# Every store through `store()` is begun by GpSimd's queue instead of SyncE's in a one-core decoder block

## The chip, the cores and the metric

The kernel runs on one core of one Trainium2 chip. The metric is the device time of one execution in microseconds (us); before the change its median over three runs is 2041.13 us. Five engines work side by side: TensorE (PE, its weight loads listed as PEld), VectorE (DVE), ScalarE (ACT), GpSimd (POOL) and SyncE (SP). A DMA is begun by an instruction in the queue of one of them and then carried out by 16 DMA engines that all queues share.

## The reference

One decoder layer for x of shape (1, 2048, 1024) in float32. Two token mixers read the same normalised input, one output projection joins them, then follows a gated feed-forward network with 2816 hidden columns:

```python
h  = rmsnorm(x, g1)
p  = h @ w_in                      # q, k, v, g, a, cb, cc, ch
la = log_sigmoid((a @ w_gate_up + b_gate)) / 16
oA = rmsnorm_head(gla_chunked(q, k, v, la)) * silu(g)   # 4 heads, 64 x 128 state
oB = cb * conv3(cc * ch)           # causal, depthwise, width 3
x1 = x + concat(oA, oB) @ w_out
h2 = rmsnorm(x1, g2)
x2 = x1 + (silu(h2 @ w_gate) * (h2 @ w_up)) @ w_down
out = rmsnorm(x2, gf)
```

`gla_chunked` carries a state over chunks: S_t = diag(exp(la_t)) S_(t-1) + k_t v_t^T, o_t = q_t S_t.

## The kernel before

The 2048 positions are four blocks of 512 (`PB`), and two blocks make a *half*. The large products (input projection, feed-forward up and down) run as *units*: a 2 x 2 arrangement of quadrants of weights and activations that is computed with seven products instead of eight, from sums and differences of the quadrants (`PRODUCTS`: A11 B11, S1 T1, S2 T2, A12 B21, S3 T3, S4 B22, A22 T4). Each float32 operand is split into a high and a low part of the type fp32r (`split`: ACT makes the high part at L194, DVE the low part at L195), so that one product over 128 rows is three matmuls, L484 to L486 in `product_step`:

```python
pe.matmul(o[:], wh, xh, ...)
pe.matmul(o[:], wh, xl, ...)
return pe.matmul(o[:], wl, xh, ...)
```

A finished bank of PSUM is copied out by ACT (L530) or added to an earlier sum by DVE (L518). The output projection (L1273 to L1276) splits its operands in the same way but is not a unit.

In the order of time the stages are: an opening up to about 50 us; the input projection of half 0 to about 250 us; that of half 1, with the recurrent mixer (GLA) in its background, to about 550 us; the output projection of half 0 and, from about 664 us, of half 1; the feed-forward network of half 0 (about 760 to 1400 us) and of half 1 (to about 2005 us); the rest is the last unit, with the final norm.

The on-chip memory does not hold the activations of a stage, so each stage writes what it makes to scratch tensors in device memory and the next reads it back in the layout that it needs:

- `siT`, `siB`: normalised inputs of the input projection, as quadrants and their sums, `op` when read back
- `sk`, `sv`, `sg`, `sd`: q and k, v, gate and decay for the GLA; `kq`, `vt`, `gt`, `ee` when read back by chunk
- `sgla`, `sm`: outputs of the two mixers, each as a high and a low part; `op` when the output projection reads them
- `sx`: x1 and the partial sums of the feed-forward part; `shT`, `shB`: normalised inputs of the feed-forward part; `sa_T`, `sa_B`: its hidden activations

Every such write goes through the helper `store` (L150), every read and every fetch of weights (`raw`) through the helper `load` (L147), and both begin the DMA on `nc.sync`, SyncE's queue:

```python
def load(dst, src):
    return nc.sync.dma_start(dst, src)
def store(dst, src):
    return nc.sync.dma_start(dst, src)
```

A queue works strictly in order: an instruction that waits holds up all behind it. A store waits until its data are computed; a load waits until the buffer that it fills is free and, if it reads a scratch tensor, until the store has landed. DMAs also share eight completion counters ("lanes") in turn, so that a DMA waits for the one eight places earlier of the same group to have landed. The order on each queue is not written by hand: the tile framework's scheduler fixes the order of each engine's instructions when the kernel is built, from its own estimate of when each can start, and sets the waits between engines.

Of 1239 DMAs that SP begins, 429 come from `store`. They are 128 rows of 2 KB each (256 KB, most of them), 128 rows of 4 KB (512 KB, `so` into `sa` and `sh`), and for `sgla` 512 rows of 512 bytes (256 KB, L1237). In the last unit the output is written by direct calls (L1579), not by `store`. GpSimd itself computes little: some masks at the start and ten operations at L1577 in the last unit.

Of the kernel before, what the change touches and what calls it, by code (L numbers as in the profile page):

```python
# [53 lines left out]
def tile_hymba_block(ctx, tc, x, xt, win, wa, wgu, wout, wffn, wdown, wdown_first, small, out):  # L54
    nc = tc.nc
    act, dve, pool, pe = nc.scalar, nc.vector, nc.gpsimd, nc.tensor
# [91 lines left out]
        return nc.sync.dma_start(dst, src)  # L148

    def store(dst, src):  # L150
        return nc.sync.dma_start(dst, src)

    last_hi, last_lo, raw_loads, last_exp = [], [], [], []
    last_out = []
# [474 lines left out]
    def opening():  # L629
# [170 lines left out]
        def out(u, j, r):  # L800
            c, acc = tt("c"), o[u, j, r]
            if j:
                queued(act, lambda: act.activation(c[:], acc[:], AF.Copy))
            else:
                queued(dve, lambda: dve.tensor_tensor(c[:], acc[:], rb0[:], ALU.mult))
            store(s_kq[j][2 * u + r][:], c[:])
# [138 lines left out]
    def h1_ahead():  # L945

        def put(n, k, h):
            if n in WHOLE:
                store(s_h1[n][k][:], h[:])
                return  # L950
            hi, lo = [bx[0].tile([P, PB], F32R, name=e, tag="b") for e in ("hi", "lo")]
            split(h[:], hi[:], lo[:])
            for e, y in enumerate((hi, lo)):
                store(s_h1[n][k][:, e, :], y[:].bitcast(F32))

        for b in (2, 3):
            rb = []
            yield from rows_rstd(squares[b][:, :, 0], rb)
            rbs[b] = rb[0]
        yield from combine(lambda k, j: xt[2 + j, :, k, :], C_G1, (rbs[2], rbs[3]), put)  # L960
# [846 lines left out]
```

## Time and profile before

| | |
|---|---|
| median of three runs | 2041.13 us |
| the three runs | 2041.13, 2042.61, 2038.8 us |
| profiled execution | 2040.97 us |
| its span in the trace | 2039.2 us |
| granted clock of TensorE, mean | 0.997 |
| DVE busy | 1534.0 us (75% of the span) |
| ACT busy | 966.0 us (47% of the span) |
| bytes moved by DMA | 422.51 MB |

The span runs from the first to the last instruction that the trace holds. The profiled execution's own time is 1.77 us longer than its span; that part lies around it. "Busy" counts the computing instructions of an engine: the instructions by which SP begins DMAs appear as rows of SPq and are not in these shares.

### The profile page before, as it was taken

What the parts mean: (1) busy time and instruction counts of PE and PEld (TensorE: products, weight loads), DVE (VectorE), ACT (ScalarE), POOL (GpSimd) and SP (SyncE); (2) the same over time, 40 slices, a digit from 0 to 9 for tenths busy, and PEclk for the clock granted to TensorE, in tenths of its full rate; (3) what the DMA queues carried; (4) which work ended last, traced back from release to release, by engine and by line L of the source; (5) the groups of instructions that cost most, each with busy time, mean ns of one, the idle gap of its engine ahead of it and who ended that gap; (6) DMA issues with size and microseconds to landing.
All of it is one profiled execution on the core that took longest, in us unless ns stands there. A gap on an engine that the chain in (4) does not pass through costs nothing.

```text
span 2039.2 us, 26918 instructions
## 1 busy us (share of the span) xinstructions
PE 2019.6 (99%) x9299; PEld 1659.4 (81%) x9299; DVE 1534.0 (75%) x2763; ACT 966.0 (47%) x1915; POOL 10.3 (1%) x17
## 2 busy tenths in 40 slices
PE   9999999999999999999999999999999999999998
PEld 8788877887888788888888888887888888888886
DVE  7888967659744697777777688887777767778886
ACT  6664455656533344444444452334534444454345
POOL 0000000000000000000000000000000000000001
PEclk9999999999999999999999999999999999999999
DMA  7356885524675983546545576577444434486653
GB/s 263 119 202 222 290 299 172 163 74 158 247 245 173 373 293 134 192 151 217 181 145 191 215 287 249 187 276 279 161 165 170 161 144 170 174 331 223 248 217 129
DMA packets 190887, 422.51 MB, mean 207 GB/s; under 512 B 20032, under 2 KB 67360, under 8 KB 181280
## 3 DMA queue, kind: packets, MB, share of 16 engines
q1 hardware_dynamic: 190032, 420.15, 58.2%
q8 instruction: 73, 1.20, 0.2%
q10 hardware_dynamic: 720, 0.66, 0.1%
q14 instruction: 62, 0.51, 0.1%
HBM read 276.02 MB, written 144.70 MB: 206 GB/s over the span
## 4 chain that ended last, share of the span: by engine, by line
PE 94%; DMA 2%; DVE 2%; ACT 1%; issue 0%; SPq 0%; POOL 0%; POOLq 0%; ACTq 0%; DVEq 0%
PE mm L484 26%; PE mm L486 26%; PE mm L485 26%; PE mm L1273 3%; PE mm L1274 3%; PE mm L1276 3%; PE a_ps L1008 1%; PE mm L789 1%; PE mm L791 1%; PE o_ps L1181 1%; PE mm L790 1%; PE mm L1594 1%; PE sc L1156 1%; PE o_ps L1188 1%; DMA op<-shT 0%; PE kv L1196 0%
## 5 line engine op out<-in xcount | busy, mean ns | idle before, releaser
L484 PE MATMUL mm<-op,wq 128*128 128x512 f32 x2443 | 951.4, 392 | 7.2 <-ACT op L194 4.1
L485 PE MATMUL mm<-op,wq 128*128 128x512 f32 x2443 | 950.2, 390 | 0.5 <-DVE op L195 0.5
L486 PE MATMUL mm<-op,wq 128*128 128x512 f32 x2443 | 940.5, 390 | 0.3
L194 ACT ACTIVATE wq<-raw 128x512 fp32r<-128x512 f32 (+2 forms) x612 | 356.8, 588 | 590.1 <-PE mm L486 469.9
L484 PEld LDWEIGHTS mm<-op,wq 128*128 128x128 f32 x2443 | 459.0, 188 | 108.8 <-ACT op L194 5.4
L486 PEld LDWEIGHTS mm<-op,wq 128*128 128x128 f32 x2443 | 458.9, 188 | 96.5 <-DVE wq L195 1.1
L485 PEld LDWEIGHTS mm<-op,wq 128*128 128x128 f32 x2443 | 459.1, 188 | 96.1 <-DVE op L195 2.4
L195 DVE TENSOR_TENSOR wq<-raw,wq 128x512 fp32r<-128x512 f32 (+2 forms) x612 | 385.4, 635 | 173.5 <-ACT wq L194 171.9
L518 DVE TENSOR_TENSOR c<-mm,c 128x512 f32<-128x512 f32 x196 | 134.7, 687 | 81.6 <-PE mm L486 72.0
L518 DVE TENSOR_TENSOR y<-mm,y 128x512 f32<-128x512 f32 x185 | 126.6, 687 | 53.8 <-PE mm L486 53.2
L530 ACT ACTIVATE c<-mm 128x512 f32<-128x512 f32 x198 | 115.4, 589 | 34.7 <-PE mm L486 30.6
L436 DVE TENSOR_TENSOR raw<-raw 128x512 f32<-128x512 f32 (+2 forms) x182 | 113.3, 628 | 2.1
L194 ACT ACTIVATE wq<-s 128x512 fp32r<-128x512 f32 (+2 forms) x96 | 56.3, 587 | 108.8 <-PE mm L486 95.7
L1273 PE MATMUL mm<-op,wq 128*128 128x512 f32 x256 | 101.1, 397 | 0.1
L1274 PE MATMUL mm<-op,wq 128*128 128x512 f32 x256 | 100.0, 391 | 0.0
L1276 PE MATMUL mm<-op,wq 128*128 128x512 f32 x256 | 82.3, 390 | 0.0
L436 DVE TENSOR_TENSOR s<-raw 128x512 f32<-128x512 f32 (+2 forms) x91 | 57.3, 629 | 27.3 <-DMA raw<-in_wffn_dram 19.7
L195 DVE TENSOR_TENSOR op<-op 128x512 fp32r<-128x512 f32 x94 | 62.1, 683 | 4.0 <-ACT op L194 3.9
L195 DVE TENSOR_TENSOR wq<-s,wq 128x512 fp32r<-128x512 f32 (+2 forms) x96 | 60.8, 633 | 1.9 <-ACT wq L194 1.0
L194 ACT ACTIVATE op<-op 128x512 fp32r<-128x512 f32 x94 | 54.9, 621 | 8.0 <-DMA op<-sa_T 4.3
L436 DVE TENSOR_TENSOR raw<-s,raw 128x512 f32<-128x512 f32 (+2 forms) x91 | 57.3, 630 | 1.3
L1273 PEld LDWEIGHTS mm<-op,wq 128*128 128x128 f32 x256 | 48.1, 188 | 11.8 <-issue 1.4
(231 smaller groups left out, 1610.2 us busy)
## 6 DMA issues: line engine op xcount, KB each, us to landing
raw<-in_wffn_dram SPq DMA_DIRECT2D x44, 1024.0 KB, 6.4
sa_B<-so SPq DMA_DIRECT2D x47, 512.0 KB, 4.2
op<-sa_B SPq DMA_DIRECT2D x47, 512.0 KB, 6.8
raw<-in_win_dram SPq DMA_DIRECT2D x22, 1024.0 KB, 5.8
sa_T<-so SPq DMA_DIRECT2D x44, 512.0 KB, 4.4
op<-sa_T SPq DMA_DIRECT2D x44, 512.0 KB, 6.7
raw<-in_wdown_dram SPq DMA_DIRECT2D x24, 768.0 KB, 5.4
sx<-y SPq DMA_DIRECT2D x48, 256.0 KB, 3.9
```

The lines of the kernel that those rows point to most:

```text
L194: last_hi[:] = [act.activation(hi, src, AF.Copy)]
L195: last_lo[:] = [dve.tensor_tensor(lo, src, hi.bitcast(F32), ALU.subtract)]
L436: dve.tensor_tensor(*args)
L484: pe.matmul(o[:], wh, xh, start=first and k == 0, stop=False, skip_group_check=True)
L485: pe.matmul(o[:], wh, xl, start=False, stop=False, skip_group_check=True)
L486: return pe.matmul(o[:], wl, xh, start=False, stop=k == n - 1, skip_group_check=True)
L518: last_plus[:] = [dve.tensor_tensor(t[:], o[:], t[:], ALU.add)]
L530: last_out[:] = [act.activation(t[:], o[:], AF.Copy)]
L789: pe.matmul(acc[:], wq[:, 0, c], p[:, 0, :], start=first, stop=False)
L1273: pe.matmul(o[e, j][:], wh, m[:, 0, :], start=k == 0, stop=False)
L1274: pe.matmul(o[e, j][:], wh, m[:, 1, :], start=False, stop=False)
L1276: pe.matmul(o[e, j][:], wl, ops[k][j][:, 0, :], start=False, stop=k == KD - 1)
```

## The change

One line. `store` begins its DMA on GpSimd's queue (`pool` is `nc.gpsimd`); `load` is left on SyncE's.

```diff
@@ -148,7 +148,7 @@
         return nc.sync.dma_start(dst, src)
 
     def store(dst, src):
-        return nc.sync.dma_start(dst, src)
+        return pool.dma_start(dst, src)
 
     last_hi, last_lo, raw_loads, last_exp = [], [], [], []
     last_out = []
```

So 429 DMAs leave SP's queue, which keeps 810, and stand in POOL's in the order in which the scheduler expects their data. The ten operations at L1577 come behind all of them. The program as built marks SP's queue as a hardware one (the page of before lists it as hardware_dynamic) and GpSimd's as not of that kind. The stores now have eight lanes of their own, and the loads keep eight.

Since the scheduler works from its own estimates, the order of other instructions changes too. Three places follow.

The first is SP's queue at the end of the input projection of half 0, about 259 to 277 us in the trace of before: `op<-siT` and `op<-siB` are operands for the products with T3, B22 and T4, `sm` takes the convolution's result, `raw<-in_win_dram` is the next unit's weights (1 MB), `gt` and `kq` are inputs of the GLA. Before:

```order
L148 DMA op<-siT_1_458 128x512
L151 DMA sm_2_203<-hi 128x512
L148 DMA op<-siT_2_459 128x512
L148 DMA op<-siT_3_460 128x512
L151 DMA sm_2_203<-c_2397 128x512
L148 DMA op<-siB_0_461 128x512
L148 DMA op<-siB_1_462 128x512
L148 DMA op<-siB_2_463 128x512
L148 DMA raw<-in_win_dram 128x2048
L148 DMA op<-siB_3_464 128x512
```

and now:

```order
L148 DMA op<-siT_1_458 128x512
L148 DMA raw<-in_win_dram 128x2048
L148 DMA op<-siT_2_459 128x512
L148 DMA op<-siT_3_460 128x512
L148 DMA op<-siB_0_461 128x512
L148 DMA gt<-sg_3_156 128x128
L148 DMA op<-siB_1_462 128x512
L148 DMA op<-siB_2_463 128x512
L148 DMA kq<-sk_0_113 128x128
L148 DMA op<-siB_3_464 128x512
```

The two `sm` stores are gone from between the operand loads, and the 1 MB fetch of weights stands ahead of six operand loads that it stood behind.

The second is the hand-off from the GLA to the output projection of half 1, about 655 to 665 us, again SP before: `sgla` is written in a high part (`gt`) and a low part (`osb`), and read back as operands.

```order
L148 DMA raw<-in_wout_dram 128x2048
L151 DMA sgla_220<-osb 512x1x128
L151 DMA sgla_220<-gt 512x1x128
L151 DMA sgla_220<-osb 512x1x128
L148 DMA op<-sgla_220 128x1024
L148 DMA op<-sgla_219 128x1024
```

and now POOL, which holds these stores:

```order
L151 DMA sx_5_174<-y 128x512
L151 DMA sx_5_182<-y 128x512
L151 DMA sgla_220<-gt 512x1x128
L151 DMA sgla_220<-osb 512x1x128
L151 DMA sgla_220<-gt 512x1x128
L151 DMA sgla_220<-osb 512x1x128
L151 DMA sx_6_175<-y 128x512
```

In both orders the last two of the four `sgla` stores come one right after the other and ahead of the first `op<-sgla` load, which now stands in another queue than they do and waits for them there.

The third is ACT near 120 us, in the input projection of half 0, where the gate's exponential (L1055) and the silu (L585) of the first outputs fall among the splits of weights (`wq`). Before:

```order
L1053 ACTIVATE em<-g_1491 128x4
L194 ACTIVATE wq<-raw 128x512
L1055 ACTIVATE el<-g_1492 128x4
L585 ACT_TABLE_LOAD
L585 ACTIVATE c_1507<-c_1507 128x512
L194 ACTIVATE wq<-s_1628 128x512
```

and now:

```order
L585 ACT_TABLE_LOAD
L585 ACTIVATE c_1507<-c_1507 128x512
L530 ACTIVATE c_1548<-mm 128x512
L608 ACTIVATE xn,ssq<-xn 128x512 x6
L194 ACTIVATE wq<-raw 128x512
L1055 ACT_TABLE_LOAD
L1055 ACTIVATE el<-g_1492 128x4
L194 ACTIVATE wq<-s_1628 128x512
L585 ACT_TABLE_LOAD
```

The first silu has moved ahead of the last exponential, so that ACT loads a function table three times there instead of once.

## The prediction

> **What bounds the kernel now.** I read the page first, for busy shares, clock and queues; then the view of waits of PE, for what it ever waits for; then, around each long wait, the chain of waits, the timelines of SP and DVE, and the table of windows, for the load on the DMA engines.
>
> ```profile
> span 2039.2 us, 26918 instructions
> PE 2019.6 (99%) x9299; PEld 1659.4 (81%) x9299; DVE 1534.0 (75%) x2763; ACT 966.0 (47%) x1915; POOL 10.3 (1%) x17
> q1 hardware_dynamic: 190032, 420.15, 58.2%
> PE mm L484 <- ACT op L194: 4.1, 2, 2.3
> PE mm L484 <- ACT c L530: 2.3, 3, 1.2
> PE rb_ps L1562 <- ACT rep L1553: 2.3, 2, 1.7
> PE mm L485 <- DVE op L195: 0.5, 2, 0.3
> ```
>
> TensorE is busy 99% of the span. No store touches it: a store can matter only where PE waits, or would wait, for something behind it. The DMA engines are used 58% on the mean, so where they matter it is by the stretch and not by the total. Of the rows of waits (in all, times, longest), rb_ps belongs to the last unit, whose stores are not moved. The others, 4.1, 2.3 and 0.5, sum to 6.9 us, and with some small ones the ceiling of what earlier stores could win is about 8 us, 0.4%. What a later store could lose has no such ceiling. About 0.2% (4.1 us) is what a measurement of this kernel can tell from no change.
>
> The sum is made against the profiled execution: 2040.97 us, of which 2039.2 is span and 1.77 lies around it. It stands 0.16 below the median of the runs, 2041.13.
>
> **Part A: the wait at 272 us.**
>
> ```profile
> 253.16 0.68 DVE L195 TENSOR_TENSOR c<-c,hi 128x512 fp32r<-128x512 f32 x1
> 265.14 5.71 DMA sm<-c
> 270.93 0.60 ACT c L530
> 272.61 0.50 PE L484 MATMUL mm<-op,wq 128*128 128x512 f32 x1 [2.32 <-ACT op L194]
> 273.43 0.50 PE L485 MATMUL mm<-op,wq 128*128 128x512 f32 x1 [0.31 <-DVE op L195]
> 272.23 0.97 SPq L151 DMA_DIRECT2D sm<-hi  x2
> 276.60 0.86 SPq L151 DMA_DIRECT2D sm<-c  x2
> 265.00:270.00 5.00, 5.00 (x24) 4.05 (x22) 0.93 (x2) 1.54 (x4) 0.00 (x0) 1.00 1.02 383
> 275.00:280.00 5.00, 5.00 (x18) 3.95 (x17) 4.97 (x9) 2.29 (x5) 0.00 (x0) 0.72 1.05 371
> ```
>
> (The last two rows: window, busy time and count by engine, then granted clock, DMA share, GB/s.) The first convolution tile's low part is done at 253.16 + 0.68 = 253.84. Its store begins only at 265.14, since SP's queue stands full of operand loads, and lands 5.71 later. That frees the buffer that ACT's copy at 270.93 needs, and the operand splits behind the copy keep PE waiting 2.32 + 0.31 = 2.6 us; the clock falls to 0.72 in the window behind, which costs up to 0.28 x 5 = 1.4 more. In GpSimd's queue nothing stands before the store, so it can go at about 254 and this stall ends: -2.6, or -4.0 with the clock.
>
> What is late next: the DMA engines are full here (share 1.02, 383 GB/s), and 256 KB take 0.26 MB / 383 GB/s = 0.68 us. The four stores of the rows at 272.23 and 276.60 would now come before the last operand loads instead of among them: 4 x 0.68 = 2.7. The order on SP also sets a 1 MB fetch of weights ahead of six operand loads, 4 x 0.68 = 2.7. If both reach PE in full, A is -2.6 + 5.4 = +2.8. I take three stores' worth, 2.0, since some of the loads land before PE needs them: **A = -0.6**, bounds -4.0 and +2.8.
>
> **Part B: the wait at 490 us.**
>
> ```profile
> 481.69 0.69 DVE g L1054
> 482.39 0.32 SPq L151
> 483.38 4.85 DMA gt<-sg
> 489.70 0.50 PE L484 MATMUL mm<-op,wq 128*128 128x512 f32 x1 [0.89 <-ACT c L530]
> ```
>
> SP's store of the decay waits for DVE's g, done at 482.38; the loads of the gate behind it go out late, and through ACT PE loses 0.89. With the store in another queue the loads do not wait for g: **B = -0.9**, bounds -0.9 and 0 (if the buffer of the gate is what they wait for next).
>
> **Part C: the hand-off of the mixer at 657 us.**
>
> ```profile
> 656.85 0.51 SPq L151 DMA_DIRECT2D sgla<-gt  x1
> 657.57 0.51 SPq L151 DMA_DIRECT2D sgla<-osb  x1
> sgla<-osb SPq DMA_DIRECT2D x1, 256.0 KB, 2.7
> 660.32 3.70 SPq L148 DMA_DIRECT2D op<-sgla  x7
> 664.32 0.39 PE L1276 MATMUL mm<-op,wq 128*128 128x512 f32 x1
> 664.79 0.47 PE L1273 MATMUL mm<-op,wq 128*128 128x512 f32 x1
> L1577 POOL TENSOR_TENSOR y<-y,ssx 128x256 f32<-128x256 f32 (+1 forms) x10 | 9.2, 949 | 2024.4 <-ACT ssx L1571 2024.4
> ```
>
> The last two stores of the GLA are begun one right after the other, at 656.85 and 657.57; the second lands 2.7 later, the first load follows at 660.32, and PE starts on it at 664.79, 0.47 after the matmul before, where the mean is 2019.6 / 9299 = 0.22. So the chain has no spare time, and what the stores lose PE loses, one for one.
>
> How long GpSimd takes to begin a DMA, before's trace does not show; it has none. Below: nothing more than SP's 0.51. Above, the nearest row is GpSimd's own operation, 949 ns at L1577: an `sgla` store is 512 rows of 512 bytes, four times the pieces of the other stores, so four such operations, 3.8. Both stores go through one queue in turn. With 0.95 each the second is issued by 656.85 + 1.9 = 658.75, 0.7 after SP's 658.08; with two operations each by 660.65, +2.6; with four by 664.45, +6.4. I take the middle one: **C = +2.6**, bounds 0 and +6.4.
>
> The Trainium skill, "DMA: Bandwidth & Descriptors", section "Anatomy of one DMA — SWDGE (gpsimd) path", has processors of GpSimd write the descriptors, and gives for such a DMA about 2.0 us plus its bytes at 436 GB/s, most of the 2.0 being the wait for the write's receipt. As an estimate from that page, 256 KB would take 2.0 + 0.6 = 2.6, which is what SP's store takes here (2.7), so by it C would be near 0 and the sum below 2.6 lower; no trace here shows a store of GpSimd yet.
>
> **Part D: the wait at 1398 us.**
>
> ```profile
> 1387.64 10.09 DMA op<-shT
> 1397.75 0.64 ACT op L194
> 1398.43 0.50 PE L484 MATMUL mm<-op,wq 128*128 128x512 f32 x1 [1.78 <-ACT op L194]
> 1379.69 0.69 DVE L518 TENSOR_TENSOR y<-mm,y 128x512 f32<-128x512 f32 x1 [0.41 <-PE mm L486]
> 1388.53 0.69 DVE L518 TENSOR_TENSOR y<-mm,y 128x512 f32<-128x512 f32 x1
> 1388.28 0.32 SPq L151 DMA_DIRECT2D sx<-y  x1
> 1398.42 0.32 SPq L151 DMA_DIRECT2D sx<-y  x1
> 1401.62 0.32 SPq L151 DMA_DIRECT2D sx<-y  x1
> 1388.00:1392.00 4.00, 4.00 (x20) 3.30 (x19) 3.02 (x5) 1.71 (x4) 0.00 (x0) 1.00 1.05 429
> ```
>
> At the change of half in the feed-forward part PE waits for an operand load that took 10.09 us because the engines are full (share 1.05, 429 GB/s). Four partial sums are finished by DVE between 1379.69 and 1388.53 (+ 0.69), but SP, busy with the loads, begins their stores from 1388.28 to 1401.62, all behind the load that PE needs. GpSimd begins them when they are ready, the first three at least 3 us before that load lands. Each is 0.26 MB / 0.41 = 0.64 us of the shared engines: three make 1.9, four 2.6, none 0 if the loads come as early as the stores because SP has less to issue. **D = +1.9**, bounds 0 and +2.6. Here the order of SP was an advantage: it kept stores that nobody waits for behind loads that PE waits for.
>
> **Part E: tables of ACT.**
>
> ```profile
> L585 ACT ACT_TABLE_LOAD x5 | 6.4, 1283 | 0.1
> 119.09 0.62 ACT L194 ACTIVATE wq<-raw 128x512 fp32r<-128x512 f32 x1
> 121.70 0.39 PE L484 MATMUL mm<-op,wq 128*128 128x512 f32 x1
> ```
>
> The new order has two more loads of function tables on ACT, both near 120 us, 1283 ns each. The split at 119.09 is done at 119.71 and PE takes its result at 121.70, 2.0 later, which covers one of them; the other has ACT's slack (busy 47%) behind it. So **E = 0**; without that cover it is 2 x 1.3 = +2.6.
>
> Everywhere else PE's order hardly moves, and a store lands well before its reader.
>
> Sum: -0.6 - 0.9 + 2.6 + 1.9 + 0 = +3.0, a span of 2042.2 and a time of 2044.0 us. All lower bounds: -4.0 - 0.9 + 0 + 0 + 0 = -4.9, 2036.1. All upper ones: 2.8 + 0 + 6.4 + 2.6 + 2.6 = +14.4, 2055.4.
>
> **The rivals.**
>
> *GpSimd's stores are slow from end to end* (slower). The place is C: if the second `sgla` store lands four operations late, +6.4, the others of the path follow.
>
> ```profile
> SPq L148 <- DMA sx<-y: 16.7, 10, 4.0
> ```
>
> Ten times SP's loads of the partial sums already wait for the landing of a store; these round trips have little spare time, and the stores at A no longer end the stall early enough. With A at 0, B at 0, D at +2.6 and C at +6.4 it is +9.0: 2050.0. It decides from about 3.8 us at C, where -1.5 + 1.9 + C passes 4.1. For it: one engine writes 429 stores that SP began in 0.3 to 0.5 us each. Against it: POOL is idle 99% of the span, and most stores have no close reader.
>
> *The waits go and nothing takes their place* (faster). SP has a third less to issue, loads go out earlier, and stores cost only what they cost now. Then A gives 4.0, B 0.9, D its 1.78 and 0.2 and C nothing: -6.9, 2034.1. For it: in A and B the store's place in SP's queue is the cause. Against it: at A and D the engines are full, and an earlier issue makes no bytes faster.
>
> *The queue doesn't matter* (no change). At A and D the same bytes pass the same engines; what goes early on one queue goes late on the other, and PE, 99% busy, sees the sum. A, C and D at 0 and B -0.9 gives 2040.1. The Trainium skill, "DMA: Bandwidth & Descriptors", section "Issuing engines are not separate DMA queues", says this of the hardware: all issuers feed the same 16 engines. The share of 1.02 to 1.05 in the windows agrees. Against it: 265.14 instead of 254 at A is a wait of the queue and not of the engines.
>
> **How the numbers follow.** The forecast, 0.42: it lies at +3.0, near the bound of 4.1, so of it 0.24 falls within 0.2%, 0.17 slower and 0.01 faster. Slow stores, 0.28, all slower. Waits go, 0.17: 0.15 faster, 0.02 within. No matter, 0.13, all within. Together faster 0.16, same 0.39, slower 0.45. Predicted 2044.0. The forecast's own range is the forecast with C from 0 to 6.4, A from -2.6 to +1, 2039 to 2049. The range reaches to the faster rival's upper half and over the slow one's 2050.0 to nearly the sum of the upper bounds, 2035.5 to 2054; about 0.1 is left out on either side.
>
> **What would show it.** In the profile of the changed kernel: POOL's instructions that begin the stores, with what one of them lasts (C: 0.95, 1.9 or 3.8 for `sgla`), and the time from issue to landing of `sgla<-osb` against 2.7. The wait of `ACT op L194` near 272 should be gone or come back under a load instead of `sm<-c`; the one near 490 gone; the gap ahead of the first L1273 of `out_proj(1)` wider by C; the wait near 1398 about 1.9 longer, behind `op<-shT` again. I am wrong on the mechanism if waits appear at places that are none of these, as inside the feed-forward stages, where `sa` goes out and comes back, or if GpSimd's queue has a backlog so that a store is issued long after its data; and wrong on the size if a store lands as fast as SP's or takes twice what I allow.

## The result and the profile after

| | before | after |
|---|---|---|
| median | 2042.19 us (6 runs) | 2056.25 us (6 runs, 2055.52 to 2056.97) |
| ratio | | 1.0071, 95% interval 1.0058 to 1.0084 |
| span of the profiled execution | 2039.2 us | 2053.8 us |
| after TensorE's last matmul, to the end of the span | 6.5 us | 12.0 us |

The change makes the kernel 0.71% slower, 14.6 us in the span. First the page of the changed kernel (its head, the queues and one group), then its view of PE's waits:

```profile
span 2053.8 us, 27177 instructions
PE 2021.2 (98%) x9299; PEld 1659.4 (81%) x9299; DVE 1535.7 (75%) x2763; ACT 968.9 (47%) x1917; POOL 247.5 (12%) x446
...
q1 hardware_dynamic: 115968, 279.62, 39.0%
q0 software_dynamic: 41168, 140.54, 18.4%
```

```profile
PE mm L484 <- DMA op<-siB: 3.1, 3, 1.3
PE mm L484 <- ACT wq L194: 2.7, 3, 1.3
PE mm L484 <- DVE c L518: 2.5, 2, 2.2
...
PE mm L485 <- DVE op L195: 1.7, 1, 1.7
...
PE mm L1273 <- DMA op<-sgla: 1.1, 2, 0.6
PE mm L1273 <- ACT q L1254: 0.8, 1, 0.8
```

The 140.54 MB of the stores are now in a queue of the software kind. PE computes nearly as long as before (2021.2 against 2019.6) and waits longer: behind `op<-siB` and `op<-sgla`, which are loads that it never waited for in before, and behind ACT's `wq` split. The waits do not give the whole difference, so I compared the start of the same matmul, counted from the first, in PE's timelines of both kernels:

| matmul starts, before | after | later by | place |
|---|---|---|---|
| 103.1 | 103.6 | 0.6 | |
| 138.1 | 141.0 | 2.9 | behind 120 us |
| 308.3 | 317.0 | 8.7 | behind the change of half in the input projection |
| 501.4 | 509.1 | 7.7 | |
| 683.6 | 693.3 | 9.7 | behind the hand-off of the mixer |
| 1416.9 | 1425.8 | 8.9 | behind the change of half in the feed-forward part |
| last one | | 9.0 | |

The first 0.6, three steps (+2.3, +5.8, +2.0) and two small returns (-1.0, -0.8) make the 9.0 us, within rounding; the other 5.6 lie after the last matmul.

The step at 280 us, in PE's timeline of the changed kernel:

```profile
269.01 0.47 PE L484 MATMUL mm<-op,wq 128*128 128x512 f32 x1 [1.29 <-DMA op<-siB]
271.27 0.50 PE L484 MATMUL mm<-op,wq 128*128 128x512 f32 x1 [1.32 <-DMA op<-siB]
276.16 0.50 PE L484 MATMUL mm<-op,wq 128*128 128x512 f32 x1 [0.50 <-DMA op<-siB]
277.49 0.50 PE L484 MATMUL mm<-op,wq 128*128 128x512 f32 x1 [0.36 <-ACT op L194]
279.71 0.69 PE L485 MATMUL mm<-op,wq 128*128 128x512 f32 x1 [1.72 <-DVE op L195]
291.73 0.47 PE L484 MATMUL mm<-op,wq 128*128 128x512 f32 x1 [2.20 <-DVE c L518]
```

and in the timelines of POOL and SP there:

```profile
257.01 0.54 POOL L151 DMA_DIRECT2D sm<-c  x1 [0.38 <-DVE c L195]
263.08 1.07 POOL L151 DMA_DIRECT2D sm<-hi  x2 [5.54 <-ACT hi L194]
264.82 1.14 POOL L151 DMA_DIRECT2D sm<-c  x2 [0.67 <-DVE c L195]
```

```profile
267.09 0.58 SPq L148 DMA_DIRECT2D raw<-in_win_dram  x1
```

The store that SP held until 265.14 now leaves at 257.01, and four more go by 266; one wait of 2.6 has become five of 5.2 in all (three behind operand loads, two behind the splits of operands) and a sixth of 2.2. The stall behind the store is gone: ACT's two copies (L530) run at 267.51 and 268.50 without waiting for an `sm` store.

The stretch at the end shows in the view of the closing code (engine, operation, count; then the shortest, median and longest in ns, and the start of the first and last), before and after:

```profile
L1802 POOLq DRAIN  x3: 34/78/1799, 2033.6 to 2039.0; - x3
```

```profile
L1802 POOLq DRAIN  x3: 40/102/10401, 2042.6 to 2053.5; - x3
L1802 SPq DRAIN  x3: 7/7/7, 2047.8 to 2053.3; - x3
```

GpSimd's first drain begins at 2042.6 in the changed kernel and lasts 10.4 us, until 2053.0. SP has seen every output land by 2047.8 and waits 5 us for it. In before that drain took 1.8.

### The profile page after: what moved, and what is told of

It is laid out like the page before. It is cut to its first block, busy times and chain, and to the rows that moved or that the text cites. A ratio compares the mean times of both kernels' runs of the same rounds, so it can differ in the third digit from the quotient of the medians.

```text
span 2053.8 us, 27177 instructions
## 1 busy us (share of the span) xinstructions
PE 2021.2 (98%) x9299; PEld 1659.4 (81%) x9299; DVE 1535.7 (75%) x2763; ACT 968.9 (47%) x1917; POOL 247.5 (12%) x446
## 2 busy tenths in 40 slices
DMA packets 157995, 422.54 MB, mean 206 GB/s; under 512 B 20032, under 2 KB 50976, under 8 KB 148384
## 3 DMA queue, kind: packets, MB, share of 16 engines
q0 software_dynamic: 41168, 140.54, 18.4%
## 4 chain that ended last, share of the span: by engine, by line
PE 76%; issue 12%; DMA 4%; DVE 3%; POOL 2%; ACT 1%; SPq 0%; POOLq 0%; ACTq 0%; DVEq 0%
PE mm L484 22%; PE mm L486 22%; PE mm L485 22%; PE mm L1273 2%; PE mm L1274 2%; PE mm L1276 2%; DMA op<-shT 1%; DMA raw<-in_win_dram 1%; PE mm L1594 1%; POOL siT L151 1%; DVE op L185 1%; PE o_ps L1181 1%; POOL siB L151 1%; DMA op<-sgla 1%; DVE h L763 0%
## 5 line engine op out<-in xcount | busy, mean ns | idle before, releaser
L484 PEld LDWEIGHTS mm<-op,wq 128*128 128x128 f32 x2443 | 459.0, 188 | 115.7 <-ACT wq L194 7.3
L486 PEld LDWEIGHTS mm<-op,wq 128*128 128x128 f32 x2443 | 459.1, 188 | 97.3 <-DVE wq L195 1.1
L485 PEld LDWEIGHTS mm<-op,wq 128*128 128x128 f32 x2443 | 459.1, 188 | 96.9 <-DVE op L195 3.9
L530 ACT ACTIVATE c<-mm 128x512 f32<-128x512 f32 x198 | 115.3, 589 | 40.5 <-PE mm L486 38.2
L151 POOL DMA_DIRECT2D sa_B<-so x47 | 25.2, 536 | 380.0 <-DVE so L195 357.9
L585 ACT ACTIVATE c<-c 128x512 f32<-128x512 f32 x78 | 48.9, 629 | 33.7 <-DVE c L518 31.4
```

Source lines behind the costliest of these rows:

```text
L151: return pool.dma_start(dst, src)
L484: pe.matmul(o[:], wh, xh, start=first and k == 0, stop=False, skip_group_check=True)
L485: pe.matmul(o[:], wh, xl, start=False, stop=False, skip_group_check=True)
L486: return pe.matmul(o[:], wl, xh, start=False, stop=k == n - 1, skip_group_check=True)
L530: last_out[:] = [act.activation(t[:], o[:], AF.Copy)]
```

## The experiments

Theory: the loss has four parts, each at a place: the order of ACT near 120 us; stores that leave early among loads at the change of half; the same at the hand-off of the mixer; the drain. The main rival: GpSimd's stores are slow, each a little, everywhere. In before and in the kernels below that leave these places as they were, the wait near 272 us took 2.6 to 3.8 and the one near 1398 us 0.5 to 2.0, so differences of 1 us at these two places mean nothing. Counted by the start of matmuls, three of these kernels come 1.0 to 2.4 us later at 272 than the profiled run of before, so of the 5.8 there some 3.4 or more belong to the change.

For the first four, `store` takes the queue as an argument, and only the named calls pass GpSimd:

```diff
-    def store(dst, src):
-        return nc.sync.dma_start(dst, src)
+    def store(dst, src, q=None):
+        return (q or nc.sync).dma_start(dst, src)
```

### One store

```diff
-            store(s_kq[j][2 * u + r][:], c[:])
+            store(s_kq[j][2 * u + r][:], c[:], pool if (j, u, r) == (0, 0, 0) else None)
```

> Before, with one single store (the first of q and k, near 60 us) begun by GpSimd; TensorE's order is that of before. Theory 'closing time is fixed': once GpSimd has begun any DMA, its closing instruction lasts about 10 us, as with all 429 stores, so the span grows by about 5.5 us (the stretch after TensorE's last matmul from 6.5 to 12 us) and all else stays. Rival 'closing time grows with the number of stores': under 0.1 us more.

Measured: 2041.23 us, ratio 0.9995 (0.9986 to 1.0005); 6.6 us after the last matmul, and the longest drain is 1893 ns. The theory of a fixed closing time falls: having used GpSimd's queue at all costs nothing.

### The feed-forward stages alone

`, pool` at L1320, L1364, L1401, L1410, L1470 and L1493, 233 DMAs.

> Only the stores of the feed-forward stages (sfT/sfB, sh, sa, sx of the down projection, out) go to GpSimd; the order of ACT keeps its table loads as before. Theory 'fixed closing time, and loss only at the two places where loads and stores meet': tail +5.5, the wait at 1398 us shorter by about 0.9, the stages before 760 us unchanged: +4.5 us in all. Rival 'every GpSimd store is slow from end to end': waits in the feed-forward stages, where hidden activations go out and come back, several us more.

Measured: 2042.28 us, ratio 1.0000 (0.9990 to 1.0009). The drain lasts 3.5 us and ends before the last output has landed, so the 5.5 us that were expected at the end do not come. The wait at 1398 us is 0.3 instead of 2.0, the stages before it are unchanged but for 1 us at 272, and no wait appears in the feed-forward stages. More than half of all the stores cost nothing: the rival falls.

### The input projection alone

`, pool` at L806, L949, L954, L1057, L1071, L1074, L1102 and L1103, 132 DMAs.

> Only the stores of the input projection (si, sk, sv, sg, sd, sm) go to GpSimd. Theory: the table loads near 120 us (+2.4) and the waits at 262 to 292 us (+6) come back in full, the tail +5.5, the hand-off at 657 us and the one at 1398 us stay as before: about +13 to +14 in the span. Rival 'the loss is a sum of small delays over all 429 stores': about half of the whole.

Measured in one run: 2050.28 us, span 2048.5. The matmuls come 2.9 us later behind 120 us and 10.4 us later behind 308 us, as in the changed kernel or somewhat more; the hand-off and the stretch at the end (6.3 us) are as in before. So two of the four parts come from these 132 stores alone; the expectation was wrong by the drain.

### Around the output projection alone

`, pool` at L1237 and L1299, 64 DMAs.

> Only the stores around the output projection (sgla, and sx of L1299) go to GpSimd. Theory: the matmuls behind the hand-off at 657 us come about 2 us later, because four sx stores now pass between the operand loads, and the tail is +5.5: about +7.5 in the span. Rival 'the two sgla stores are begun late': +0.4 at the hand-off (two times 0.72 instead of 0.51 us to begin one) and no more; +6.

Measured in one run: 2045.24 us, span 2043.2, 4.0 above that of before. The matmuls behind the hand-off come 1.6 us later than those ahead of it, some 2 us came at 272, where this kernel has the order of before, and the stretch at the end is 6.5. The 2 us at the hand-off were expected, the 5.5 at the end were not to be found.

### The order of ACT put back

```diff
-        act.activation(el[:, i, :], dd[:, :, P - 1], AF.Exp, scale=1.0 / 16.0)
+        last_el[:] = [act.activation(el[:, i, :], dd[:, :, P - 1], AF.Exp, scale=1.0 / 16.0)]
...
-        last_silu[:] = [act.activation(s[:], c[:], AF.Silu)]
+        with behind(last_el if len(decays) < 3 else []): last_silu[:] = [act.activation(s[:], c[:], AF.Silu)]
```

> The changed kernel (all stores on GpSimd), with the first silu held behind the last exponential of the gate, so that ACT loads 15 tables again instead of 17; SP's order is that of the changed kernel. Theory 'the matmuls come 2.4 us later near 120 us because of the order of ACT, not because of the queue': the two waits of PE at 123 and 125 us (0.38 and 1.30) go, and all later matmuls come about 2.4 us earlier: about 2054. Rival 'those waits come from late stores': no change there, 2056.

Measured: 2054.28 us against 2056.25 of the changed kernel; the matmul at 138.1 us is 0.6 late instead of 2.9, and the two waits of PE are gone. The stores are where they were, so this part belongs to the order that the scheduler chose and not to the queue.

### The fetch of weights put back

```diff
-        raw_loads.append(load(raw, src))
+        with behind([und_loads[6]] if len(raw_loads) == 11 else []): raw_loads.append(load(raw, src))
```

(`und_loads` are the operand loads of T3, B22 and T4; the seventh is `op<-siB_2_463`.)

> The changed kernel, with the 1 MB fetch of weights at 267 us put back behind the operand loads on SP; the sm stores still leave early through GpSimd. If the place of the fetch on SP causes the waits of PE between 265 and 292 us (7.4 and the matmuls 6 us late), they fall to about 3 or less and the time to about 2052. If the five early stores cause them, they stay within 1.5 us of what they are: about 2055 to 2056.

Measured: 2053.93 us. PE's waits at the place:

```profile
269.86 0.47 PE L484 MATMUL mm<-op,wq 128*128 128x512 f32 x1 [0.87 <-DMA op<-siB]
272.11 0.64 PE L484 MATMUL mm<-op,wq 128*128 128x512 f32 x1 [1.33 <-DMA op<-siB]
279.12 0.49 PE L484 MATMUL mm<-op,wq 128*128 128x512 f32 x1 [0.37 <-ACT op L194]
281.33 0.50 PE L485 MATMUL mm<-op,wq 128*128 128x512 f32 x1 [1.72 <-DVE op L195]
```

The wait of 2.20 at 291.73 is gone, the others remain with 4.3 of 5.2. The result lies between the two expectations: the early fetch makes the last wait, and what makes the first five is something else.

### The sm stores put back

All stores on GpSimd but those of L1102 and L1103; SP's order at the place is that of before.

> The changed kernel, with the sm stores alone back on SP; SP's order from 259 to 277 us is then that of before. If either the early stores or the fetch of weights cause the late matmuls at 265 to 292 us, both are undone: the waits go back to those of before (2.6 to 3.7, behind the store sm<-c), the matmuls come 4 to 6 us earlier, about 2051. If GpSimd's other stores (si, sk, sd) cause them, nothing changes: 2056.

Measured: 2049.24 us, ratio to before 1.0034 (1.0023 to 1.0046).

```profile
268.81 0.50 PE L484 MATMUL mm<-op,wq 128*128 128x512 f32 x1 [0.25 <-DMA op<-siB]
277.53 0.64 PE L484 MATMUL mm<-op,wq 128*128 128x512 f32 x1 [3.66 <-ACT op L194]
```

The waits behind `op<-siB` shrink to 0.25, and what is left is the wait of before. With the run before it, which has the fetch back too but the `sm` stores early: the early `sm` stores make the first five waits, the early fetch the sixth. The hand-off costs 2.9 us in this run, against 2.0 in the changed kernel. The drain lasts 7.9 us instead of 10.4, with 397 DMAs instead of 429.

### Nothing else on GpSimd at the end

```diff
-            scale("j0", d, pool, sp)
+            scale("j0", d, dve, sp)
...
-            scale("p0", d, pool, sp)
+            scale("p0", d, dve, sp)
...
-            scale("p1", d, pool, ac)
+            scale("p1", d, dve, ac)
```

> The changed kernel, with the ten multiplications of the last unit that GpSimd does (L1577) given to DVE, so that GpSimd's last instruction before its closing drain is a store near 2000 us. If the drain (10.4 us in the changed kernel, ending 5 us after SP has seen every output land) waits only on GpSimd's own earlier work, it is over long before the end: the stretch after the last matmul falls from 12.0 to 7 to 8 us (DVE has six more operations of 0.38 us in line), about 2052. If it waits for the other engines or for the end of all DMAs, it stays at 12 us or more: 2056.

Measured: 2054.6 us, span 2052.2.

```profile
L1802 POOLq DRAIN  x3: 45/93/9203, 1840.7 to 2052.0; - x3
```

The drain takes 9.2 us, but from 1840.7, behind the last store, where it delays nobody. The stretch at the end is 6.8 us instead of 12.0: the drain waits only for GpSimd's own work, and its 5 us can be hidden. DVE's added work gives 2.2 us of it back in the last unit (PE waits 1.84 and 1.50 where it waited 0.63 and 0.51).

### The sx stores put back

All stores on GpSimd but those of L1299.

> The changed kernel, with the 32 sx stores of the output projection (L1299) back on SP, behind the operand loads; the sgla stores stay with GpSimd. Theory 'four sx stores pass between the operand loads at the hand-off': the three waits of PE there (0.84, 0.59, 0.46) shrink to under 0.7 in all and the matmuls behind come 1.5 to 2 us earlier; the drain lasts as long as with the sm stores back (397 stores too, 7.9): about 2051. Rival 'the two sgla stores are begun late': the waits stay, and only the drain is shorter: about 2053.

Measured in one run: 2053.09 us, span 2051.4. Of the three waits at the hand-off only the first is left:

```profile
672.17 0.47 PE L1273 MATMUL mm<-op,wq 128*128 128x512 f32 x1 [0.84 <-ACT q L1254]
```

The matmuls behind the hand-off come 0.4 us later than those ahead of it, against 2.0 in the changed kernel. The two `sgla` stores are where they were, so by this one run the `sx` stores made 1.6 of the 2.0. The wait that is left belongs to the `sgla` stores, as part C below shows. The drain is 7.8 us with 397 DMAs. The time as a whole missed the expectation because the wait near 1400 us took 2.45 here.

### ACT's queue for the sm stores

The `sm` stores by ACT, everything else as in before.

> Before, with the sm stores alone begun by ACT, whose queue is of the hardware kind; nothing on GpSimd. SP's order has the 1 MB fetch ahead of the operand loads here too. Theory 'what costs is that stores leave early and the fetch stands early, not that GpSimd writes the descriptors': waits behind op<-siB appear between 262 and 292 us as in the changed kernel, 3 to 6 us more than in before, about 2044 to 2047, with no longer closing drain. Rival 'the software queue costs': no such waits, the wait on the store sm<-c goes, about 2038 to 2039.

Measured: 2058.96 us, ratio 1.0082 (1.0068 to 1.0096). It tells the two theories apart less well than it was meant to:

```profile
261.83 0.33 ACTq L151 DMA_DIRECT2D sm<-hi  x1
265.71 0.33 ACTq L151 DMA_DIRECT2D sm<-c  x1
266.14 0.42 ACT L1143 ACTIVATE ee<-ee 128x256 f32<-128x256 f32 x1 [13.30 <-DMA op<-siB]
```

```profile
268.11 0.79 PE L484 MATMUL mm<-op,wq 128*128 128x512 f32 x1 [8.80 <-DVE c L518]
```

ACT made `hi` by 252.8 but begins its store only at 261.83, and does nothing for 13.3 us: the store shares the eight lanes with SP's loads and waits for one (that of a `vt<-sv` load, which landed at 261.75), and ACT's computing stands behind it. On GpSimd, until the last unit, only other stores stand behind a store that waits; here PE lost 8.8 us. Whether a hardware queue without that wait would spare the loads stays open.

### Only the stores that SP held up

From before: one `sm<-c` (the first of the half-0 pair at 254 us), the `sd` of half 1 and the `sx` of L1470 on GpSimd, 21 DMAs; the fetch of weights pinned as above.

> Before, with only those stores on GpSimd that SP held up at the three waits: one sm<-c at 254 us, the decays of half 1 (sd), and the partial sums of the down projection (sx, L1470); the 1 MB fetch is held in its old place. Theory 'a store that leaves early helps where a buffer waits for it and costs only by the bytes that it puts ahead of loads': one store at 272 us (0.7 of engine time for 2.6 to 3.9 of waiting), -0.9 at 490, -1 to -1.6 at 1398: 4 to 6 us less, about 2036 to 2038. Rival 'the buffers are then held by the next store of the same tiles, still on SP': under 2.5 us less, 2039.5 to 2042.

Measured: 2039.2 us, ratio 0.9986 (0.9977 to 0.9995), the only kernel here that is faster than before, by less than the 0.2% that can be told. At the first two places nothing was won that can be told:

```profile
273.15 0.50 PE L484 MATMUL mm<-op,wq 128*128 128x512 f32 x1 [2.47 <-ACT op L194]
489.13 0.50 PE L484 MATMUL mm<-op,wq 128*128 128x512 f32 x1 [0.87 <-ACT c L530]
```

At the first place the store of the low part is out of the way. ACT's timeline shows what it waits for now:

```profile
270.46 0.60 ACT L530 ACTIVATE c<-mm 128x512 f32<-128x512 f32 x1 [4.24 <-DMA sm<-hi]
...
272.47 2.70 ACT L194 ACTIVATE op<-op 128x512 fp32r<-128x512 f32 x5
```

The store of the high part, which this kernel leaves on SP, is begun at 263.12 and holds the copy until 270.46, as the rival of the expectation has it. The product that is copied was done at 269.32, so this store costs at most 1.1 of the 2.5; the rest is ACT's own work, two copies and two splits of weights ahead of the split that PE waits for. So the run does not show what moving both stores would win without the rest of the change. (The chain of waits names a load there, `op<-siB` from 269.14 to 273.21. It cannot be the cause of the wait: ACT begins to split the operand at 272.47.) At the second place the wait is that of before, and part B below shows what makes it.

### Three things put back

Tables, `sm` stores and the `sx` stores of L1299 together; 365 DMAs stay with GpSimd.

> The changed kernel, with three things undone together: the table loads of ACT as before (the silu held behind the exponential), the sm stores and the sx stores of the output projection back on SP. 365 stores stay with GpSimd. Theory 'the loss is the sum of tables (2.4), early sm stores with the early fetch (4 to 6), sx stores between the operand loads (1.5 to 2), and the closing drain': TensorE's last matmul comes within 1.5 us of where it is before; the drain, shorter by 2.5 us for each 32 stores taken away so far, ends some 3.5 us after GpSimd's last operation, before or about when the last output has landed, so that it costs under 1: 2041 to 2043. If stores on GpSimd cost anything at other places, 2044 or more.

Measured: 2046.3 us, ratio 1.0021 (1.0011 to 1.0030). Of the 14 us, 10 are undone. The last matmul comes 3.7 us later than in before instead of 9.0: 1.1 by 138 us, 2.6 at the change of half (a wait of 1.19 behind `op<-siB` and 3.29 where before had 2.32), 1.2 at the hand-off, less returns of 1.2 in all elsewhere. The drain takes 6.2 us, 4.5 of them behind GpSimd's last operation, and costs 1.4. By the expectation's own bounds stores on GpSimd cost something at other places too: the four parts are the bulk of the loss, and not all of it. The 2.6 are hardly more than the 2.4 by which unchanged kernels differ at that place, and whether the other early stores of the input projection (`si`, `sk`) make the wait of 1.19 was not tried. The 1.2 come without the `sx` stores of the output projection, in one wait of 1.67; the `sgla` stores are still on GpSimd.

## Why the prediction was wrong

The direction was right, "slower" with 0.45, and the time was not: 2044.0 with a range to 2054, measured 2056.25. The direction owes something to luck: most of the loss lies in part A, in part E and at the end, which stood in the sum at -0.6, 0 and nothing, and the 1.9 of part D did not come. Step by step:

- **Part A** (-0.6, bounds -4.0 and +2.8; measured +5.8) failed in both of its terms. The gain of 2.6 took the whole wait at 272 us for the store's, since the chain of waits named it. ACT's timeline of before shows how little of it was:

```profile
270.93 0.60 ACT L530 ACTIVATE c<-mm 128x512 f32<-128x512 f32 x1 [0.83 <-DMA sm<-c]
271.42 0.62 ACT L194 ACTIVATE wq<-raw 128x512 fp32r<-128x512 f32 x1
271.94 1.66 ACT L194 ACTIVATE op<-op 128x512 fp32r<-128x512 f32 x3
```

  ACT was idle for only 0.83 before the copy, and the copy also needs PE's product, which was done at 272.61 - 2.32 = 270.29. Without the store it could have begun about 0.6 earlier (an estimate from these rows); the rest of the 2.6 is the copy and two splits, one after the other on ACT. The loss had the right mechanism and the wrong size: "I take three stores' worth, 2.0, since some of the loads land before PE needs them". Little was covered. Both sources that I had summed to 5.4 came, with 7.4 of waits: five of 5.2 for the early stores and 2.2 for the early fetch.
- **Part B** (-0.9; measured 0) ended at its upper bound, and its chain was misread. The wait of 0.89 is there unchanged in the changed kernel. In before ACT works without a pause from here to the copy at 489.06 that PE waits for:

```profile
488.01 1.15 ACT L194 ACTIVATE hi<-c 128x512 fp32r<-128x512 f32 x2 [0.39 <-DVE c L1098]
```

  It begins when DVE's L1098 is done. The load of the gate landed at 488.23 (483.38 + 4.85), when ACT was already at work, so an earlier load would not have moved the copy.
- **Part C** (+2.6; measured +2.0) was nearly the right number with a part of the cause. I priced the begin of an `sgla` store on GpSimd at 1.9 us. It takes 0.72, and the store lands nearly as fast as SP's:

```profile
L151 POOL DMA_DIRECT2D sgla<-osb x16 | 11.6, 727 | 8.3 <-DVE osb L195 7.9 <-issue 0.2
```

```profile
665.56 3.04 DMA sgla<-osb
```

  3.04 from begin to landing, against 2.7. Behind it the operand loads begin:

```profile
668.75 3.76 SPq L148 DMA_DIRECT2D op<-sgla  x7
```

  The matmuls ahead are 7.7 late, so 668.75 is 661.0 in before's time, 0.7 behind before's 660.32, and PE's wait of 0.84 at 673.26 follows. The view puts that wait down to ACT's `q`, but in before the same matmul (664.79) did not wait for that `q`, which was done at 665.46; in both kernels it starts 0.13 to 0.14 after the first of these loads has landed (673.13 and 664.65). So the path of part C is there, at about a third of its price, and it is the wait that stays when the `sx` stores go back. The other two waits, 0.59 and 0.46, go with the four `sx` stores that leave at 671 to 674 us among the operand loads; their mechanism is that of the loss in part A, which I had not looked for here. The Trainium skill, "DMA: Bandwidth & Descriptors", section "Anatomy of one DMA — SWDGE (gpsimd) path", whose figures give an estimate of 2.6 us for such a store, was nearer to the 3.04 than my rows.
- **Part D** (+1.9; measured -0.8 over the feed-forward stages) saw one effect and missed what stands against it. The load that PE waits for takes longer, 14.45 us instead of 10.09, with the stores among the loads:

```profile
1392.26 14.45 DMA op<-shT
1406.70 0.02 issue
1406.73 0.64 ACT op L194
```

  It also begins earlier. The matmuls ahead are 9.6 us late here, so 1392.26 is 1382.7 in before's time, 5.0 us ahead of 1387.64: SP has no stores between its loads, and the loads have eight lanes to themselves. That this is why was not tried. The load lands 0.6 earlier, and PE waits 1.11 instead of 2.0. That is within the 0.5 to 2.0 of this place, and with the partial sums on GpSimd the wait was 0.3 in one run and 2.45 in another, so neither a loss nor a gain is shown here.
- **Part E** (0; measured +2.3) failed in the cover. I counted the two table loads against 2.0 us of slack. In the new order the split stands behind a silu, the first table load and six row statistics as well:

```profile
116.23 1.28 ACT L585 ACT_TABLE_LOAD   x1
117.53 0.63 ACT L585 ACTIVATE c<-c 128x512 f32<-128x512 f32 x1
...
122.22 0.62 ACT L194 ACTIVATE wq<-raw 128x512 fp32r<-128x512 f32 x1
122.86 1.28 ACT L1055 ACT_TABLE_LOAD   x1
```

  The split that ran at 119.09 runs at 122.22, the next one, behind the second table load, at 124.27, and PE waits 0.38 at 122.89 and 1.30 at 124.94. All these rows stood in the new order that was known before the run, and I counted only two of them.
- **The end of the kernel** (measured +5.6) was in no part and no rival. I took the last unit for untouched because its stores are not moved, and did not ask what GpSimd does before the kernel can end.

Of the rivals, slow stores fell (0.54 us to begin one, a landing of 3.04 against 2.7, nothing lost by 233 of them). That all waits go fell with part A. That the queue doesn't matter is true of the 233 feed-forward stores, whose kernel stands at 1.0000, and not of the change of half in the input projection and the hand-off of the mixer.

## What to carry to other kernels

A queue that holds loads and stores in order can also protect the loads: where the DMA engines are full, a store that leaves when its data are ready can take its bytes' time from a load that somebody waits for. Before moving DMAs to another queue, look in each full stretch for what will go out earlier there, and at the very end for what that engine must finish before the kernel may close. When a chain of waits names one releaser, ask which release would have come next and when, and price the gain by that distance (about 0.6 us at 272, not 2.6): look at how long the engine that was held stood idle, and not only at PE's wait. And when a scheduler re-orders, count every row that comes to stand ahead of the one that is waited for.

## What the hardware showed that was not expected

- The closing drain of GpSimd depends on what it has begun, and not in a simple way. With 0, 1, 21, 64, 132, 233, 365, 397 and 429 DMAs it lasted 1.8, 1.9, 3.5, 4.4, 3.9, 3.5, 6.2, 7.8 to 7.9 and 10.4 us, some 1.7 of each spent on GpSimd's own last operations; with 429, it lasted 9.2 where GpSimd had been idle. It was 10.4 in each of three kernels with 429. In the changed kernel GpSimd had stood idle for 192 us between its last store and its operations of the last unit, so the drain is not time of stores only just begun. What it does in that time was not settled.
- GpSimd begins a store of 128 rows in 0.54 us and one of 512 rows in 0.72, where SP takes 0.32 and 0.51, while DVE is busy 75% of the span.
- The same bytes go in fewer packets: 157995 packets for 422.54 MB instead of 190887 for 422.51. The kernel did not become faster by it.
